# Two operand parts in one 512-column product, output groups of 256 columns, halves summed at evacuation

## The chip, the cores and the metric

The kernel runs on one core of a Trainium2 chip. The metric is the device time of one execution, in microseconds (us), as a median of several runs. TensorE (PE) does the matrix products, VectorE (DVE) and ScalarE (ACT) everything elementwise, GpSimd (POOL) a few small things, and SyncE (SP) issues most of the transfers.

## The reference, cut to what matters

Three transformer blocks run in sequence on one sequence of 256 tokens with 2048 features: two layers of `first_block` and one block of a second kind. Each block has a mixer and a feed-forward part, with a norm and a residual around each:

```python
h = rmsnorm(x, g_pre_mix[l])
proj = h @ w_in[l]                      # 2048 x 4608
y_a = conformer_conv(proj[..., :a_end], ...)
y_b = dilated_attention(proj[..., a_end:b_end], cos, sin)
y_c = pool_mixer(proj[..., b_end:], ...)
y = concat(rms_normalize(y_a), rms_normalize(y_b), rms_normalize(y_c)) * g_mix[l]
x = x + rmsnorm(y @ w_out[l], g_post_mix[l])
h = rmsnorm(x, g_pre_ffn[l])
f = (silu(h @ w_gate[l]) * (h @ w_up[l])) @ w_down[l]      # hidden 5632
x = x + rmsnorm(f, g_post_ffn[l])
```

The third block has the same form with other branches (a linear recurrent unit, a gated delta rule, spatial gating, a short convolution) and a feed-forward part with a convolution of three taps. All data are float32, and the weights (some 590 MB) are read from HBM once.

## The kernel before

**Layout.** Activations lie with features on partitions and 256 tokens along the free axis. A float32 product is made of three products of reduced-precision parts: every weight and every operand is split into a high and a low part, and hi x hi, hi x lo and lo x hi are added up in PSUM. `mms` (L332) does this for one weight tile of 128 x 128: three products of 256 columns (L340, L341, L342), each with a weight load of its own (the first two load the same weights).

**Weights.** `Stream` (L58) cuts the weights into chunks of 512 x 512, each in two halves of 256 rows by 512 columns (512 KB; rows of 2 KB in DRAM). For each half chunk SP issues a load (L79), ACT rounds it to the high part (L87), DVE subtracts to get the low part (L95). `ahead` emits this three half chunks before the products want it; the low parts rotate through four buffers.

**Groups.** `groupA` (L364) computes 512 output features: four tiles of 128 x 256, two in each of two PSUM banks, over its chunks. With K = 2048 a group has 8 half chunks; in the mixer's output products (`oc`, `oa`) it has only 2, in `ob` 4. `dualA` (L404) runs two such groups together at the start of each half block; `groupB` (L385) has tokens on the output's partitions and products of 512 columns (L396 to L398).

**Work beside the products.** All engines follow one order of emission, and each engine takes its own instructions in that order. After every half chunk `pump` (L154) emits work from generators, with a credit of `BUDGET` = 1450 ns of VectorE time per half chunk; what is not used is lost, what is overdrawn is carried on. First come the `hot` generators, then the evacuations of finished groups (`evq`, in order), then the background generators `bg` in their order, each as long as credit is left. A generator yields the time of what it has just emitted; a negative value rests until the next half chunk. `new_ps` (L355) emits, before a new group, whatever is left of the evacuations up to two groups back. `drain` (L195) emits all that is left of the evacuations and of the named generators at once, with no products in between.

**The mixer of a Block1 layer** (L845) runs `dualA` for a and gate, then `pool`, `v0`, `q0`, `q1`, `k0`, `k1`, `v1` (8 half chunks each), `oc` (4 groups), `drain(conv)` (L911), `oa` (4 groups, operand yA), `drain(at)` (L914), `ob` (4 groups, operand yb). Beside them run `conv_gen` (31 taps, then `ln_gen` L571, then `y_gen` L601, which writes yA), `pool_gen`, two `rot_gen`, and `attn_gen` (L731): eleven steps of 900 ns of credit each, one a half chunk at most, each with the reductions of pair s, the scaling of s - 1, the transposes of s - 2 and the product with the values of s - 3. `attn_gen` stands ahead of `conv_gen` in `bg`.

**Feed forward** (`ffn_run` L1027): eleven hidden groups with a gate and an up product, and three passes of down products over hidden groups 0 to 3, 4 to 7 and 8 to 10; `act` (L1048) emits what is left of the evacuation of a hidden group when its product is due. `last_group` and `fin_last` (L935, L957) end a half block with the sums for the norm.

Of the kernel before, what the change touches and what calls it, by code (L numbers as in the profile page):

```python
# [17 lines left out]
P = 128  # L18
# [13 lines left out]
class Params:  # L32
    """Columns of the packed per-feature parameters: name -> (first, count)."""
# [27 lines left out]
class Stream:  # L61
    """Weight chunks of 512 rows by 512 columns, loaded ahead by halves and split into two 12-bit parts."""
# [4 lines left out]
    def __init__(self, net, plan):  # L67
        self.net, self.plan = net, plan
        self.n = 2 * len(plan)
        self.nd = self.nhi = self.nlo = 0  # L70
        self.i = 0
        self.st, self.hi, self.lo = {}, {}, {}

    def _dma(self):
        h = self.nd
        net = self.net
        ap = self.plan[h // 2][1][256 * (h % 2):256 * (h % 2) + 256, :]
        t = net.wst.tile([P, 2, 512], F32, tag="st", name="st")
        net.nc.sync.dma_start(out=t, in_=ap.rearrange("(k p) c -> p k c", p=P))  # L79
        self.st[h] = t  # L80
        self.nd += 1

    def _hi(self):
        h = self.nhi
        net = self.net
        hi = net.whl.tile([P, 2, 512], F32R, tag="hi", name="whi", bufs=self.SA + 2)
        net.nc.scalar.copy(hi, self.st[h])  # L87
        self.hi[h] = hi
        self.nhi += 1

    def _lo(self):
        h = self.nlo
        net = self.net
        lo = net.whl.tile([P, 2, 512], F32R, tag="lo", name="wlo", bufs=self.SA + 1)
# [4 lines left out]
    def ahead(self, i):  # L99
        """Everything emitted that the products of half chunk i and those soon after it want."""  # L100
# [10 lines left out]
    def get(self, key, b):  # L111
        i = self.i
        assert self.plan[i // 2][0] == key and i % 2 == b, (self.plan[i // 2][0], key, i, b)
        self.ahead(i)
        self.i += 1
        return self.hi.pop(i), self.lo.pop(i)


class Net:
    def __init__(self, ctx, tc, ins, out, taps=None):  # L120
# [16 lines left out]
        self.lag = 0  # L137
# [12 lines left out]
    # Generators emit a few instructions and yield their VectorE time in ns, less the TensorE time that  # L150
    # they add; a negative value rests until half a chunk of products later.
# [33 lines left out]
    def flush(self, gid=None):  # L185
        """Emit all that is left of the evacuations up to group `gid`."""
# [8 lines left out]
    def drain(self, *gens):  # L195
        """Emit all that is left of these background generators (of all, if none is named)."""
# [12 lines left out]
    def after(self, gen, ev):  # L209
        """The evacuation `ev`, once the background generator `gen` is through."""  # L210
        def e(ps):
# [6 lines left out]
            yield from ev(ps)  # L218
# [8 lines left out]
    def setup(self):  # L227
        """First what the first products want: a gain, and rows of x in turn with the first weights."""
# [33 lines left out]
    def stat_mm(self, ps, accs, start=True, stop=True):  # L262
        """Sums over features of [128, 256] tiles, tokens on partitions, into ps[:, 0:2]."""
# [5 lines left out]
    def stat(self, accs, n, name="r"):  # L269
        """rsqrt(sum over features / n + eps), tokens on partitions: [128, 2]."""  # L270
# [21 lines left out]
    def rsqrt_fast(self, src, scale, n, name="r"):  # L292
        """The same from ScalarE's square root and one Newton step, where the products wait for it."""
# [11 lines left out]
    def load_sqrt(self):  # L305
        """ScalarE's table of square roots, before it is wanted."""
# [3 lines left out]
    def bcast(self, r, name="R"):  # L310
        """[128 tokens, 2] -> PSUM [128, 256], the same row on every partition."""
# [20 lines left out]
    def mms(self, ps, j, hi, lo, k, act, first, last):  # L332
        """One 128x128 weight tile times 256 tokens, features on the output's partitions."""
        nc = self.nc
        if len(ps) == 2:
            o, head, tail = ps[j // 2][:, j % 2, :], j % 2 == 0, j % 2 == 1
        else:
            o, head, tail = (ps[0][:, j, :], j == 0, j == 1) if j < 2 else (ps[j - 1], True, True)
# [4 lines left out]

    def mms_first(self, ps, hi, lo, acts):
        """The first half chunk's products, in the order in which their operands are ready."""
# [9 lines left out]
    def new_ps(self, shape=(P, 2, T)):  # L355
        self.gid += 1
        self.flush(self.gid - 2 - self.lag)
        self.lag = 0
# [5 lines left out]
    def groupA(self, keys, act, evac=None, now=None):  # L364
        """Chunks `keys` (4 row tiles each) of one 512-column group; act(k) -> (hi, lo).

        evac(ps): generator over both pairs of output tiles; now(j, ps): at once, when output tile j is
        complete (tiles 0 and 1 share a bank and are complete together: j = 1)."""
        ps = self.new_ps()
        if now:  # L370
            ps = [ps[0], ps[1][:, 0, :], self.bank("ps_mm", (P, 2, T))[:, 0, :]]
        nh = 2 * len(keys)
        for h in range(nh):
            hi, lo = self.W.get(keys[h // 2], h % 2)
            for j in range(4):
                for k in range(2):
                    self.mms(ps, j, hi, lo, k, act(2 * h + k), h == 0 and k == 0, h == nh - 1 and k == 1)
                if now and h == nh - 1 and j:
                    now(j, ps[j - 1])
            if evac and h == nh - 1:  # L380
                self.later(evac(ps))
# [1560 lines left out]
```

## Time and profile before

| | us |
|---|---|
| median of 3 runs (lowest, highest) | 3457.39 (3457.18, 3462.28) |
| span of the profiled execution | 3458.9 |
| PE busy | 3423.8 |
| PE weight loads (beside the products) | 3365.6 |
| DVE busy | 2180.8 |
| ACT busy | 1648.5 |
| POOL busy | 105.0 |
| HBM traffic, mean | 176 GB/s |

The profiled execution's span is 1.5 us above the median. The end of a product in the profile is modelled and products overlap, so the cost of one is read from the distance of their starts. A DVE or ACT instruction overlaps its neighbour by some 0.07 us in the same way.

### The profile page before, as it was taken

How to read it: one execution, taken by the hardware profiler on the slowest of the kernel's cores; microseconds unless marked ns; L12 is line 12 of the kernel's file. 1: busy time of each engine (PE TensorE's matmuls, PEld its weight loads, DVE VectorE, ACT ScalarE, POOL GpSimd, SP SyncE). 2: the span in 40 equal slices, each digit the busy share in tenths (PEclk: the TensorE clock that was granted, in tenths of full speed). 3: DMA queues.
4: the chain of work that ended last, by engine and by line, in shares of the span. 5: the costliest groups of instructions: out<-in, count | busy, mean ns of one | idle time of the engine just before them, and what ended most of it. 6: DMA issues, size and time to landing. Idle time of an engine off the chain costs nothing.

```text
span 3458.9 us, 66199 instructions
## 1 busy us (share of the span) xinstructions
PE 3423.8 (99%) x27758; PEld 3365.6 (97%) x27758; DVE 2180.8 (63%) x2957; ACT 1648.5 (48%) x2219; POOL 105.0 (3%) x301
## 2 busy tenths in 40 slices
PE   9999999999999999999999999999999999999999
PEld 9989999999999998999999999999999999999998
DVE  6877755455555787775545555578665766466465
ACT  5556544444344555554444334455435554455344
POOL 0000000000000000000000000001110000000000
PEclk9999999999999999999999999999999999999999
DMA  7654566666665565456666666565435665666563
GB/s 234 185 170 142 169 184 183 184 183 184 183 183 182 162 190 164 157 157 186 183 183 181 186 183 183 178 189 165 128 122 190 179 184 184 183 183 182 185 184 130
DMA packets 315436, 609.44 MB, mean 176 GB/s; under 512 B 19168, under 2 KB 24672, under 8 KB 314880
## 3 DMA queue, kind: packets, MB, share of 16 engines
q1 hardware_dynamic: 314224, 599.37, 57.9%
q0 software_dynamic: 912, 5.83, 0.5%
q8 instruction: 217, 3.56, 0.4%
q14 instruction: 83, 0.68, 0.1%
HBM read 598.84 MB, written 6.29 MB: 175 GB/s over the span
## 4 chain that ended last, share of the span: by engine, by line
PE 95%; DVE 2%; POOL 1%; DMA 1%; issue 0%; ACT 0%; SPq 0%; DVEq 0%; POOLq 0%; ACTq 0%
PE ps_mm L340 29%; PE ps_mm L342 29%; PE ps_mm L341 29%; PE ps_st L266 1%; PE ps_mm L352 1%; PE ps_mm L396 1%; PE ps_mm L397 1%; PE ps_mm L398 1%; PE ps_sc L747 0%; PE ps_av L794 0%; DVE wlo L95 0%; PE ps_pt L782 0%; PE ps_bc L314 0%; POOL q L287 0%; POOL q L286 0%
## 5 line engine op out<-in xcount | busy, mean ns | idle before, releaser
L95 DVE TENSOR_TENSOR wlo<-st,whi 128x1024 fp32r<-128x1024 f32 x1120 | 1365.8, 1222 | 923.0 <-PE ps_mm L342 839.4
L87 ACT CAST whi<-st 128x1024 fp32r<-128x1024 f32 x1120 | 1170.5, 1049 | 1250.7 <-PE ps_mm L341 1084.6
L340 PE MATMUL ps_mm<-hhi,whi 128*128 128x256 f32 x5712 | 1621.0, 284 | 0.1
L341 PE MATMUL ps_mm<-hlo,whi 128*128 128x256 f32 x5712 | 1616.6, 283 | 0.1
L342 PE MATMUL ps_mm<-hhi,wlo 128*128 128x256 f32 x5712 | 1616.5, 283 | 0.3 <-DVE wlo L95 0.3
L340 PEld LDWEIGHTS ps_mm<-hhi,whi 128*128 128x128 f32 x5712 | 1096.5, 192 | 1.2 <-issue 0.3
L341 PEld LDWEIGHTS ps_mm<-hlo,whi 128*128 128x128 f32 x5712 | 1096.5, 192 | 0.6 <-DVE hlo L480 0.3
L342 PEld LDWEIGHTS ps_mm<-hhi,wlo 128*128 128x128 f32 x5712 | 1096.4, 192 | 0.6 <-DVE wlo L95 0.5
L340 PE MATMUL ps_mm<-hid,whi 128*128 128x256 f32 x2112 | 597.9, 283 | 0.0
L342 PE MATMUL ps_mm<-hid,wlo 128*128 128x256 f32 x2112 | 597.7, 283 | 0.0
L341 PE MATMUL ps_mm<-hid,whi 128*128 128x256 f32 x2112 | 597.7, 283 | 0.0
L340 PEld LDWEIGHTS ps_mm<-hid,whi 128*128 128x128 f32 x2112 | 405.5, 192 | 0.0
L341 PEld LDWEIGHTS ps_mm<-hid,whi 128*128 128x128 f32 x2112 | 405.5, 192 | 0.0
L342 PEld LDWEIGHTS ps_mm<-hid,wlo 128*128 128x128 f32 x2112 | 405.5, 192 | 0.0
L342 PE MATMUL ps_mm<-y,wlo 128*128 128x256 f32 x448 | 127.4, 284 | 3.8 <-DVE wlo L95 3.8
L340 PE MATMUL ps_mm<-y,whi 128*128 128x256 f32 x448 | 129.9, 290 | 0.0
L341 PE MATMUL ps_mm<-y,whi 128*128 128x256 f32 x448 | 127.3, 284 | 0.0
L340 PEld LDWEIGHTS ps_mm<-y,whi 128*128 128x128 f32 x448 | 86.4, 193 | 4.8 <-issue 2.0
L342 PEld LDWEIGHTS ps_mm<-y,wlo 128*128 128x128 f32 x448 | 86.5, 193 | 4.2 <-DVE wlo L95 4.2
L341 PEld LDWEIGHTS ps_mm<-y,whi 128*128 128x128 f32 x448 | 86.6, 193 | 0.1
L1019 ACT CAST hid<-su 128x512 fp32r<-128x512 f32 x66 | 40.7, 621 | 88.0 <-DVE su L1018 88.0
L474 ACT ACTIVATE hhi<-x,par 128x256 fp32r<-128x256 f32 x84 | 38.2, 501 | 91.9 <-DVE x L468 91.0
(413 smaller groups left out, 2672.7 us busy)
## 6 DMA issues: line engine op xcount, KB each, us to landing
st<-in_w_in_dram SPq DMA_DIRECT2D x232, 512.0 KB
st<-in_w_gate_dram SPq DMA_DIRECT2D x176, 512.0 KB
st<-in_w_up_dram SPq DMA_DIRECT2D x176, 512.0 KB
st<-in_w_down_dram SPq DMA_DIRECT2D x176, 512.0 KB
st<-in_ffn_up_dram SPq DMA_DIRECT2D x176, 512.0 KB
st<-in_w_out_dram SPq DMA_DIRECT2D x96, 512.0 KB
st<-in_ffn_down_dram SPq DMA_DIRECT2D x88, 512.0 KB
xpark<-x POOLq DMA_DIRECT2D x1, 2048.0 KB, 6.9
```

What stands on the lines that cost most here:

```text
L87: net.nc.scalar.copy(hi, self.st[h])
L95: net.nc.vector.tensor_tensor(lo, self.st.pop(h), self.hi[h], ALU.subtract)
L266: self.nc.tensor.matmul(ps[:, t:t + 1], a[:, t * P:(t + 1) * P], self.ones[:, 0:1], start=start and i == 0 and t == 0, stop=stop and i == ...
L340: nc.tensor.matmul(o, hi[:, k, w], act[0], start=first and head, stop=False)
L341: nc.tensor.matmul(o, hi[:, k, w], act[1], start=False, stop=False)
L342: nc.tensor.matmul(o, lo[:, k, w], act[0], start=False, stop=last and tail)
L352: mm(ps[j // 2][:, j % 2, :], w[:, k, j * P:(j + 1) * P], acts[k][a], start=n == 0 and k == 0 and j % 2 == 0, stop=False)
L396: nc.tensor.matmul(ps[t], a[0][:, ts], hi[:, k, :], start=h == 0 and k == 0, stop=False)
L397: nc.tensor.matmul(ps[t], a[0][:, ts], lo[:, k, :], start=False, stop=False)
L398: nc.tensor.matmul(ps[t], a[1][:, ts], hi[:, k, :], start=False, stop=h == nh - 1 and k == 1)
L474: nc.scalar.activation(hhi[:, k, :], x[:, k, :], AF.Identity, scale=self.p(g, k))
L1019: nc.scalar.copy(h[:, 0, sl, :], u[:, sl, :])
```

## The change

Wherever `groupA` runs, the high weights now meet both parts of the operand at once: one product of 512 columns writes hi x hi into the first half of a bank and hi x lo into the second; lo x hi is a product of 256 columns added to the second half. Each output tile of 128 features so takes a whole bank, a group has 256 output features instead of 512 (two tiles, two banks, half the half chunks), and the evacuation adds the two halves: two ACT copies of 128 x 256, a rest until the next half chunk, two DVE additions of 128 x 256. `dualA`, `groupB` and the very last 256 columns of each half block keep products of 256 columns. The half chunks of `groupA` become 512 rows by 256 columns (rows of 1 KB in DRAM, the same 512 KB). The operand's parts are stored side by side per row tile. Evacuations run pair by pair with rests in them; `hid_gen` rests between the copy of the high part and the subtraction. `BUDGET`, the order of the stages, the drains and the generators of conv, pool, attention and the delta rule are as before.

```diff
+def by_cols(chunks):
+    return [(key, c, ap[:, 256 * c:256 * c + 256], 4) for c in range(2) for key, ap in chunks]

+    def mms_wide(self, o, j, hi, lo, k, act, first, last):
+        mm = self.nc.tensor.matmul
+        w = slice(j * P, (j + 1) * P)
+        mm(o, hi[:, k, w], act[2], start=first, stop=False)
+        mm(o[:, T:], lo[:, k, w], act[0], start=False, stop=last)

+    def take(self, dst, src):
+        if not isinstance(src, list):
+            nc.scalar.copy(dst, src)
+            yield 50
+            return
+        for j in range(2):
+            nc.scalar.copy(dst[:, j, :], src[j][:, 0:T])
+        yield 50
+        yield -1
+        for j in range(2):
+            nc.vector.tensor_tensor(dst[:, j, :], dst[:, j, :], src[j][:, T:], ALU.add)
+        yield 850
+
+    def scaled(self, dst, src, R):
+        if isinstance(src, list):
+            yield from self.take(dst, src)
+            src = dst
+        self.nc.vector.tensor_tensor(dst, src, self.b2(R, dst.shape[1]), ALU.mult)
+        yield 600
+
+    def added(self, dst, src):
+        if not isinstance(src, list):
+            V.tensor_tensor(dst, dst, src, ALU.add)
+            yield 600
+            return
+        for c in (slice(0, T), slice(T, 2 * T)):
+            for j in range(2):
+                V.tensor_tensor(dst[:, j, :], dst[:, j, :], src[j][:, c], ALU.add)
+            yield 850

     def groupA(self, keys, act, evac=None, now=None):
-        ps = self.new_ps()
...
+        n = len(keys)
+        for c in range(2):
+            one = now is not None and c == 1
+            ps = self.new_ps((P, 512))
...
+            for h in range(n):
+                hi, lo = self.W.get(keys[h], c)
+                for j in range(2):
+                    for k in range(4):
+                        mms(ps[j], j, hi, lo, k, act(4 * h + k), h == 0 and k == 0, h == n - 1 and k == 3)
...
+                if h == n - 1 and not one:
+                    self.later(evac(c, ps))
+                self.pump()

     def hk(self, k):
-        return self.hhi[:, k, :], self.hlo[:, k, :]
+        h, k = self.h[k // 8], k % 8
+        return h[:, k, 0, :], h[:, k, 1, :], h[:, k, :, :]

-        def ev_c(cg):
-            def ev(ps):
-                for i in range(2):
-                    nc.scalar.copy(self.f[:, 4 * cg + 2 * i:4 * cg + 2 * i + 2, :], ps[i])
-                    yield 50
-        def ev_a2(cg):
-            def ev(ps):
-                for i in range(2):
-                    o = self.f[:, 4 * cg + 2 * i:4 * cg + 2 * i + 2, :]
-                    V.tensor_tensor(o, o, ps[i], ALU.add)
-                    yield 600
+        ev_c = lambda cg: (lambda i, src: self.take(fpair(cg, i), src))
+        ev_a2 = lambda cg: (lambda i, src: self.added(fpair(cg, i), src))

+    def hid_gen(self, hid, j, i, u, s):
+        V.tensor_tensor(u, u, s, ALU.mult)
+        nc.scalar.copy(h[:, 0, sl, :], u)
+        yield 600
+        yield -1
+        V.tensor_tensor(h[:, 1, sl, :], u, h[:, 0, sl, :], ALU.subtract)
+        yield 600
```

## Rows read from the trace of the kernel before

**Rows 1.** The page, busy time and share of the span, instructions.
```profile
PE 3423.8 (99%) x27758; PEld 3365.6 (97%) x27758; DVE 2180.8 (63%) x2957; ACT 1648.5 (48%) x2219; POOL 105.0 (3%) x301
```
**Rows 2.** Groups of TensorE by line and shape: count, busy us, mean ns | idle before.
```profile
L340 PE MATMUL ps_mm<-hhi,whi 128*128 128x256 f32 x5712 | 1621.0, 284 | 0.1
...
L340 PE MATMUL ps_mm<-hid,whi 128*128 128x256 f32 x2112 | 597.9, 283 | 0.0
...
L340 PE MATMUL ps_mm<-y,whi 128*128 128x256 f32 x448 | 129.9, 290 | 0.0
...
L340 PE MATMUL ps_mm<-yb,whi 128*128 128x256 f32 x256 | 72.9, 285 | 0.0
...
L340 PE MATMUL ps_mm<-yA,whi 128*128 128x256 f32 x64 | 18.1, 283 | 0.0
```
**Rows 3.** Timeline at 1000 us, products of 256 columns: start us, us, instruction.
```profile
1000.10 0.28 PE L340 MATMUL ps_mm<-hhi,whi 128*128 128x256 f32 x1
...
1000.46 0.28 PE L340 MATMUL ps_mm<-hhi,whi 128*128 128x256 f32 x1
```
**Rows 4.** Timeline at 85 us, products of 512 columns (`groupB`), seven apart.
```profile
84.72 0.39 PE L396 MATMUL ps_mm<-whi,hhi 128*128 128x512 f32 x1
...
86.31 0.39 PE L397 MATMUL ps_mm<-wlo,hhi 128*128 128x512 f32 x1
```
**Rows 5.** Groups by line and shape, 195 to 300 us; the last of the page.
```profile
L805 DVE TENSOR_TENSOR yacc<-yacc,ysq 128x256 f32<-128x256 f32 x6 | 2.6, 425 | 2.7 <-ACT ysq L804 2.7
...
L804 ACT ACTIVATE ysq<-ps_av 128x256 f32<-128x256 f32 x6 | 2.3, 385 | 3.5 <-DVE yb L799 3.5
...
L618 DVE TENSOR_TENSOR cs<-cs,ps_bc 128x1024 f32<-128x1024 f32 x1 | 1.2, 1215 | 0.0
...
L609 DVE TENSOR_TENSOR yacc<-yacc,t 128x512 f32<-128x512 f32 x1 | 0.7, 693 | 0.1
L607 ACT ACTIVATE yacc<-cs 128x512 f32<-128x512 f32 x1 | 0.6, 630 | 0.4 <-DVE cs L596 0.4
...
L95 DVE TENSOR_TENSOR wlo<-st,whi 128x1024 fp32r<-128x1024 f32 x1120 | 1365.8, 1222 | 923.0 <-PE ps_mm L342 839.4
```
**Rows 6.** Timeline of PE, one attention step's products between those of `oa`.
```profile
267.23 1.08 PE L794 MATMUL ps_av<-ring,v 128*64 128x256 f32 x8
268.25 1.09 PE L782 MATMUL ps_pt<-ident,ring 128*128 128x128 f32 x8
269.27 1.13 PE L747 MATMUL ps_sc<-k,q 64*128 64x256 f32 x8
```
**Rows 7.** Timeline of DVE, the first instructions of three attention steps.
```profile
269.27 0.17 DVE L768 RECIPROCAL as<-as 128x4 f32<-128x4 f32 x1
269.48 1.14 DVE L772 TENSOR_SCALAR ring<-ring,as 128x256 f32<-128x256 f32 x4
...
275.62 0.18 DVE L768 RECIPROCAL as<-as 128x4 f32<-128x4 f32 x1 [1.02 <-ACT ring L762]
...
282.11 0.17 DVE L768 RECIPROCAL as<-as 128x4 f32<-128x4 f32 x1
```
**Rows 8.** The chain that ended last, stretches of it: start us, us, what.
```profile
55.88 0.80 PE ps_st L266 x8
...
62.79 0.71 PE ps_bc L314 x4
```
**Rows 9.** The chain at the end of the conv branch in layer 0.
```profile
223.27 1.07 ACT cs L595
...
224.37 1.23 DVE cs L596
225.59 1.14 DVE wlo L95
```
**Rows 10.** Stretches (us): busy PE, PEld, DVE, ACT, POOL, clock, DMA share, GB/s.
```profile
14.00:15.00 1.00, 1.00 (x11) 1.00 (x10) 1.00 (x2) 0.78 (x1) 0.00 (x0) 1.00 1.08 383
...
357.00:362.00 5.00, 4.79 (x27) 4.77 (x28) 4.25 (x11) 1.36 (x3) 0.00 (x0) 0.65 0.00 0
...
600.00:750.00 150.00, 150.00 (x1252) 150.00 (x1251) 69.95 (x63) 61.55 (x65) 0.00 (x0) 1.00 0.62 184
...
2342.00:2365.00 23.00, 23.00 (x194) 23.00 (x194) 22.93 (x30) 11.74 (x15) 0.00 (x0) 1.00 0.55 161
```

More of the change, by code (lines that the diff above doesn't have):

```diff
@@ L217, in e @@
                 self.drain_only(gen)
-            yield from ev(ps)
+            yield from ev(*src)
         return e
@@ L364, in groupA @@
     def groupA(self, keys, act, evac=None, now=None):
-        ps = self.new_ps()
[L370 to L381, printed above, removed]
-            self.pump()
+        n = len(keys)
+        for c in range(2):
+            one = now is not None and c == 1
+            ps = self.new_ps((P, 512))
+            if one:
+                ps = [b[:, 0:T] for b in ps]
+            mms = self.mms_one if one else self.mms_wide
+            for h in range(n):
[3 more added lines that the diff above has]
+                        mms(ps[j], j, hi, lo, k, act(4 * h + k), h == 0 and k == 0, h == n - 1 and k == 3)
+                    if one and h == n - 1:
+                        now(j, ps[j])
+                if h == n - 1 and not one:
+                    self.later(evac(c, ps))
+                self.pump()
         return self.gid
@@ L428, in dualA @@
                     if end:
-                        self.evq.append((gids[s], (evac0, evac1)[s](ps[s])))
+                        ev = (evac0, evac1)[s]
+                        for pair in range(2):
+                            self.evq.append((gids[s], ev(pair, ps[s][pair])))
                     self.pump()
-        self.lag = 1
+        self.lag = [1, 1]
         return gids
@@ L687, in qk_evac, with ev @@
     def qk_evac(self, dst, base):
-        nc = self.nc
-        def ev(ps):
-            for i in range(2):
-                k = base + 2 * i
-                nc.vector.tensor_tensor(dst()[:, k:k + 2, :], ps[i], self.b2(self.R), ALU.mult)
-                yield 600
+        def ev(i, src):
+            k = base + 2 * i
+            yield from self.scaled(dst()[:, k:k + 2, :], src, self.R)
         return ev
@@ L937, in last_group, with ev @@
         nc = self.nc
-        if cg < 3:
-            def ev(ps):
-                for i in range(2):
-                    k = 4 * cg + 2 * i
-                    add(self.f[:, k:k + 2, :], ps[i])
-                    self.sq_add(self.f[:, k:k + 2, :], nc.vector)
-                    yield 1200
-                    self.gains(k)
-            self.groupA(keys, act, self.after(gen, ev) if gen else ev)
-        else:
+        def ev(i, src):
+            k = 4 * cg + 2 * i
+            yield from add(self.f[:, k:k + 2, :], src)
+            self.sq_add(self.f[:, k:k + 2, :], nc.vector)
+            yield 600
+            self.gains(k)
+        if cg == 3:
             self.load_sqrt()
-            self.groupA(keys, act, now=lambda j, ps: self.fin_last(j, ps, add))
+        self.groupA(keys, act, self.after(gen, ev) if gen else ev,
+                    now=(lambda j, ps: self.fin_last(j, ps, add)) if cg == 3 else None)
     def gains(self, upto):
@@ L1053, in act @@
                     self.flush(gids[j])
-                return hid[j][:, 0, k % 4, :], hid[j][:, 1, k % 4, :]
+                return self.yk(hid[j], k % 4)
             def ev(cg):
-                def e(ps):
-                    for i in range(2):
-                        o = f[:, 4 * cg + 2 * i:4 * cg + 2 * i + 2, :]
-                        if first:
-                            nc.scalar.copy(o, ps[i])
-                            yield 50
-                        else:
-                            V.tensor_tensor(o, o, ps[i], ALU.add)
-                            yield 600
-                return e
-            add = lambda o, ps: V.tensor_tensor(o, o, ps, ALU.add)
+                to = self.take if first else self.added
+                return lambda i, src: to(f[:, 4 * cg + 2 * i:4 * cg + 2 * i + 2, :], src)
             for cg in range(4):
@@ L1361, in ba_gen @@
         yield -1
-        ps = self.bank("ps_ba")[:, 0:T]
+        ps = self.bank("ps_ba")
         for k in range(KD):
```

430 lines of the change are left out of this document (200 added, 230 removed).

## The prediction

> **What bounds the kernel now.** I read the page first: PE is busy 99% of the span, DVE 63%, ACT 48% [rows 1]. So the question is what one product costs. The groups of TensorE show that nearly all of PE's work is the three lines of `mms`, with almost no idle time before them [rows 2]; the duration there is modelled, so I go to the timeline. Three products of 256 columns take 0.36 us from start to start, 0.120 each [rows 3]. In `groupB` the same kernel runs products of 512 columns: seven take 1.59 us, 0.227 each [rows 4]. Twice the columns cost 107 ns more, so a product of 256 columns has 107 ns of columns and 13.3 ns (120 - 107) that come once per product whatever its width. That fixed part is what the change can save. Then I read who waits for whom: DVE's weight split waits 839 us in all for PE to give back a buffer [rows 5]. DVE is thus held about one half chunk ahead of PE by the four buffers, and work that `pump` emits after half chunk i runs about while PE does half chunk i. Last I read the stretches of the mixers, where DVE is nearly full or where drains stand.
>
> **What the change saves.** A weight tile goes from 3 x 0.120 = 0.360 us to 0.227 + 0.120 = 0.347 us: one fixed part of 13.3 ns less, the columns being the same 768. The tiles of `mms` are 5712 + 2112 + 448 + 256 + 64 = 8592 [rows 2]. Not changed are the tiles of the six `dualA` (128 tiles each, 48 of them in `mms_first`, so 720 here) and of the last 256 columns of each half block (72 of hid, 32 of yb, 16 of y and yA: 120). That leaves 7752 tiles x 13.3 ns = **103 us**. The weight loads stay hidden: at 512 columns they have more cover than now.
>
> Here the Trainium skill speaks against the change. "TensorE: Matmul & The Clock Gate", section "Back-to-back issue gap", puts a product at N / 2.4 + 2.5 ns, 109 ns for 256 columns and 216 for 512, so the fixed part would be 2.5 ns and the saving 19 us. The rows differ from it (120 and 227), and the sum goes by the rows.
>
> **Evacuations.** Each pair of tiles gets two DVE additions of 128 x 256 more, 2 x 0.425 us, and ACT copies at about 0.385 each [rows 5]. `groupA` evacuates 292 pairs in all (98 in each of the two layers, 96 in the third block), of which 6 are narrow: 286 x 0.85 = 243 us more on DVE. 2181 + 243 over about 3400 is 71% of the span, so over the whole DVE does not become the bound. In the feed forward it is at 47% [rows 10] and has room: no cost there. In the mixers the extra work is not a matter of busy time but of credit.
>
> **The drains of the Block1 mixers.** The pump gives 1450 ns per half chunk. An evacuated pair in `pool`, `q0`, `q1`, `k0`, `k1` now costs 50 + 850 + 600 = 1500 instead of 600: ten pairs, 9000 ns, over six half chunks of credit, and conv is last in the queue. Its taps so end about 8 half chunks later, at the end of `v1`. In `oc` (8 half chunks, 11,600 ns) the eight pairs cost 900 each instead of 50, 7200; attention is next and gets four steps (3600), where it gets eight now; conv gets the rest, overdrawn. At `drain(conv)` 4800 ns of conv are left: the tanh, and all of `y_gen`. In `oa` the eight pairs want 1700 each, 13,600 against 11,600: attention gets nothing, and at `drain(at)` seven of its eleven steps are left. Before, the same count gives a conv that ends one half chunk before `oa` and an attention that ends with the last half chunk of `oa`; the attention steps in the trace stand where this count puts them, one or two half chunks apart [rows 6, 7]. `oa` needs yA, `ob` needs yb, and a drain emits no products, so what is drained stands in PE's way.
>
> *drain(conv)*, from the last product of `oc`: ACT copies of the last pair 0.77 (they wait for that product and stand before the tanh in ACT's queue); tanh 1.07 and DVE 1.23 [rows 9]; two squares 1.26, their sum 0.69 [rows 5]; sums on PE, GpSimd's inverse root and the broadcast 62.79 + 0.71 - 55.88 = 7.62 [rows 8]; DVE 1.22 [rows 5]; the first high and low part, about 1.0. Sum 14.9 us, of which 1.5 is PE's own work that it does today too: 13.4 us idle. After a shorter pause, PE's clock was granted at 0.65 in the mean over 5 us, between the levels of 1.2 and 2.4 GHz, and 27 products took 4.79 us instead of 3.24 [rows 10]: 1.6 more. **15 us** a layer.
>
> *drain(at)*: first the last pair's four additions, 4 x 0.425 = 1.7. A step cannot be faster than its own loop (scale on DVE, reduce on DVE, exponentials on ACT, next scale): the steps' first instructions lie 6.35 and 6.49 us apart where PE had only some 6.0 of work [rows 7]. Four of the seven steps have this loop, 25.6 us; then scale 1.35, transposes 1.09, copies 1.2, values 1.08 for the last pair, 4.7. Sum 32.0. PE's own part is 3.1 for a full step [rows 6], 4 x 3.1 + 2 x 2.1 + 1.05 = 17.6, which it does today too. Idle 14.4, restart 1.6: **16 us** a layer. Both drains in two layers: **62 us**. Today the end of conv (ACT 1.07, DVE 1.23) holds back a weight split and PE for some 2 us a layer [rows 9]; that wait goes into the drain: -3.7.
>
> **Smaller terms.** (a) The last down pass has three half chunks per group, and hidden group 10 is wanted at the third, two after its evacuation began (now four). With the new rests the subtraction is still to be emitted, behind a weight split that waits for PE: 1.2 [rows 5] + 0.7 less 0.7 of products before it, about 1.3 in two halves; with the convolution four taps, a product, a copy and a subtraction, about 4: **7 us**. (b) In the third block, DVE is full at 2342 to 2365 [rows 10]. Two pairs more there (1.7) and a stage 3.7% shorter (0.9) have to show: 2.6, and as much beside it; taken as **5**, ends 0 and 12. (c) Sums and broadcast lie two half chunks apart, 5.55 us instead of 5.76, against 6.1 needed [rows 8]: **2**. (d) Rows of 1 KB: the loads of x are such rows, and at 14 to 15 us they landed at 383 GB/s [rows 10]; the stream takes 184, about 190 after: no cost, covered by the buffers ahead. If that cover went, DMA would bound at far more than this rate, so nothing is added.
>
> The split of a moving operand into two stretches of 256 columns (for y and hid) is not in the trace. Bounds: 0 as in [rows 4], or a whole fixed part, which would take the 103 us back. I take 0, since the columns still come one after another into one bank.
>
> **Sum** against the profiled execution: 3458.9 - 103 + 62 - 3.7 + 7 + 5 + 2 = 3428. The median lies 1.5 below that execution: **3427 us**, 0.9% faster, where the products alone would give 3.0%.
>
> **Rivals.** *The drains are mostly hidden.* For it: DVE and ACT run ahead of PE, and the chain may begin while the last group's products run. Against it: both begin behind evacuations that wait for PE's last product. With a third of the 62 left the time is 3457 - 103 + 21 + 10 = 3385. Chance 0.25 for 3360 to 3404.
>
> *The drains cost more than the products save.* The mechanism: with no products between them PE's clock falls, the steps' own products take twice as long and come into the loop, and the splits that follow are late. The point is 47 us a layer for both drains instead of 31; at 56 the time is 3478. For it: the clock row [rows 10]. Against it: 3.1 us of a step's 6.4 is PE's, beside the loop. Chance 0.09.
>
> *The product of 512 columns doesn't save what it should*: the fixed part is paid per 256 columns of the moving operand. Then nothing is saved and the time is 3457 + 72 = 3529. Against it: [rows 4]. Chance 0.03. A milder form, in which the fixed part is only some 2.5 ns and most of the 13.3 goes with the columns, saves 19 and gives 3457 - 19 + 72 = 3510; [rows 3, 4] speak against it too. Chance 0.02. This milder form is the rule of the Trainium skill's "TensorE: Matmul & The Clock Gate" cited above.
>
> *No change that can be measured* (some 0.2%, 7 us, is what a measurement of this kernel can tell): drains at about 45 a layer, 3450 to 3464. Chance 0.09. My forecast, 3405 to 3450, has 0.52.
>
> **How the numbers follow.** Faster 0.52 + 0.25 = 0.77; same 0.09; slower 0.14. The range leaves out the lower end of the first rival and most of the slower cases: 3372 to 3470.
>
> **What would show it.** Starts of PE in a wide group 0.227 and 0.120 apart, 2 per tile (right), or 0.24 (wrong). In each Block1 mixer two idle stretches of PE: 13 us before the first product with yA, and before the first with yb some 32 us with attention products alone. If these are shorter than 5 us, my count of credit or of cover is wrong and the time lies near 3385; if PE idles for DVE's splits through the mixers, the additions were not hidden. In the feed forward no new wait but one of a few us before hidden group 10.

## The result and the profile after

The changed kernel takes 3514.1 us (median of 4 runs, 3506.47 to 3522.86) against 3457.28 before (4 runs, 3455.14 to 3462.28). The ratio is 1.0158, 95% interval 1.0134 to 1.0181: slower by 1.6%, where 0.9% faster was forecast, and outside the range of 3372 to 3470. The profiled execution has a span of 3504.8 us.

The page of after, busy time of each engine with its share of the span, and then its groups of instructions (busy us, mean ns | idle time before them and what ended it), answering [rows 1] and [rows 2, 5]:

```profile
span 3504.8 us, 51460 instructions
PE 3384.7 (97%) x19942; PEld 2962.4 (85%) x19942; DVE 2394.8 (68%) x3604; ACT 1757.0 (50%) x2608; POOL 106.3 (3%) x301
...
L96 DVE TENSOR_TENSOR wlo<-st,whi 128x1024 fp32r<-128x1024 f32 x1120 | 1365.3, 1223 | 716.9 <-PE ps_mm L367 490.9
L366 PE MATMUL ps_mm<-h,whi 128*128 128x512 f32 x4992 | 1763.9, 398 | 0.0
L367 PE MATMUL ps_mm<-h,wlo 128*128 128x256 f32 x4992 | 1402.1, 281 | 6.3 <-DVE wlo L96 6.3
L366 PE MATMUL ps_mm<-hid,whi 128*128 128x512 f32 x2040 | 718.8, 397 | 7.3 <-DVE hid L1063 7.3
L366 PE MATMUL ps_mm<-y,whi 128*128 128x512 f32 x440 | 161.9, 409 | 4.7 <-DVE y L688 4.7
```

TensorE is idle 120 us now (3504.8 - 3384.7), 35 before (3458.9 - 3423.8). VectorE has 214 us more to do (2394.8 against 2180.8 in [rows 1]; 243 were forecast).

The product pairs (a pair of products is here the one of 512 and the one of 256 columns of one weight tile) come at two paces. The timeline of TensorE (start, modelled duration), first in the first block's feed forward, then in the third block's, answering [rows 3, 4]:

```profile
999.72 0.40 PE L366 MATMUL ps_mm<-h,whi 128*128 128x512 f32 x1
999.96 0.28 PE L367 MATMUL ps_mm<-h,wlo 128*128 128x256 f32 x1
1000.08 0.40 PE L366 MATMUL ps_mm<-h,whi 128*128 128x512 f32 x1
1000.32 0.28 PE L367 MATMUL ps_mm<-h,wlo 128*128 128x256 f32 x1
1000.43 0.40 PE L366 MATMUL ps_mm<-h,whi 128*128 128x512 f32 x1
...
3099.91 0.39 PE L366 MATMUL ps_mm<-h,whi 128*128 128x512 f32 x1
3100.14 0.28 PE L367 MATMUL ps_mm<-h,wlo 128*128 128x256 f32 x1
3100.26 0.39 PE L366 MATMUL ps_mm<-h,whi 128*128 128x512 f32 x1
3100.49 0.28 PE L367 MATMUL ps_mm<-h,wlo 128*128 128x256 f32 x1
3100.60 0.39 PE L366 MATMUL ps_mm<-h,whi 128*128 128x512 f32 x1
```

Two pairs take 0.71 us in the first stretch and 0.69 in the second. To see it precisely, take a whole pass of down products (32 half chunks of 8 pairs): 90.5 us in the first two blocks and 88.7 in the third, so 353.3 or 346.7 ns a pair. The second is the forecast's 347; the first saves half as much. The 0.24 from a product of 512 columns to the next start, which the prediction named as the sign of a wrong price, stands in the first stretch. The windows of the same kernel (stretch, its length, then busy us and count of PE, PEld, DVE, ACT, POOL, and the granted clock) say that no clock is behind it: it is full in both.

```profile
600.00:700.00 100.00, 100.00 (x568) 86.73 (x567) 54.10 (x62) 44.44 (x56) 0.00 (x0) 1.00 0.58 186
3100.00:3200.00 100.00, 100.00 (x579) 88.16 (x578) 74.66 (x106) 56.16 (x82) 0.00 (x0) 1.00 0.62 188
```

What TensorE waited for, in four stretches of after: from `oc` to the first products with yb in the first layer; the end of `ob`; gq to gz of the third mixer (the four input groups of its delta rule); the last down pass of the third block (total us, times, longest). Here ps_av is attention's product with the values, ps_st are the sums for a norm, ps_bc is the broadcast of its factor, sqacc are the squares that the closing norm sums up:

```profile
PE ps_av L851 <- ACT ring L841: 10.8, 6, 2.7
PE ps_st L278 <- DVE yacc L671: 6.6, 1, 6.6
PE ps_bc L326 <- POOL r_y L301: 4.0, 1, 4.0
PE ps_mm L366 <- DVE y L688: 2.4, 1, 2.4
...
PE ps_st L278 <- DVE sqacc L583: 5.7, 1, 5.7
...
PE ps_mm L367 <- DVE wlo L96: 5.5, 2, 3.4
PE ps_st L278 <- DVE yacc L671: 5.3, 1, 5.3
...
PE ps_mm L366 <- DVE hid L1063: 4.8, 1, 4.8
```

The three waits ahead of the first yA product (6.6 + 4.0 + 2.4) are the drain of conv, the ps_av waits that of attention. From the last product with yA to the first with yb 34.9 us pass in each layer, with attention's products alone, where the prediction named some 32. The other two places were not in the forecast, or far too small there.

**The account.** I took the start of every half chunk from both traces (narrow: three products of 256 columns per weight tile; wide: one of 512 and one of 256) and split each stage's time into a nominal part (2.880 us per narrow half chunk, 2.720 in `groupB`, 2.773 per wide one), the excess of wide half chunks that run at 2.827, and the rest, "stalls" (waits, other products, and half-clock stretches behind a wait). The sum closes on the spans' difference of 45.9 us:

| us, after less before | forecast | measured |
|---|---|---|
| products at 346.7 ns a pair | -103 | -103.4 |
| the part of them that ran at 353.3 | 0 | +31.6 |
| `oc` and `oa`, two layers (drains less the old conv stall) | +58 | +67.6 (32.9 and 34.7) |
| last down passes (hidden group 10) | +7 | +8.6 (1.1, 1.4, 6.1) |
| third mixer | +5 | +23.2 (17.7 of it in gq to gz) |
| `ob`, two layers | 0 | +17.2 (8.7 and 8.5) |
| everything else | +2 | +0.9 |
| sum | -31 | +45.7 |

### The profile page after: what moved, and what is told of

It is laid out like the page before. It is cut to its first block, busy times and chain, and to the rows that moved or that the text cites. A ratio compares the mean times of both kernels' runs of the same rounds, so it can differ in the third digit from the quotient of the medians.

```text
span 3504.8 us, 51460 instructions
## 1 busy us (share of the span) xinstructions
PE 3384.7 (97%) x19942; PEld 2962.4 (85%) x19942; DVE 2394.8 (68%) x3604; ACT 1757.0 (50%) x2608; POOL 106.3 (3%) x301
## 4 chain that ended last, share of the span: by engine, by line
PE 88%; DVE 6%; POOL 2%; ACT 2%; issue 1%; DMA 0%; SPq 0%; DVEq 0%; POOLq 0%; ACTq 0%
PE ps_mm L366 48%; PE ps_mm L367 24%; PE ps_mm L350 2%; PE ps_mm L351 2%; PE ps_mm L349 2%; DVE wlo L96 2%; PE ps_mm L460 1%; PE ps_mm L461 1%; PE ps_mm L462 1%; POOL q L298 1%; PE ps_st L278 1%; PE ps_mm L413 1%; POOL q L299 1%; PE ps_bc L326 1%; ACT ring L819 0%
## 5 line engine op out<-in xcount | busy, mean ns | idle before, releaser
L366 PE MATMUL ps_mm<-h,whi 128*128 128x512 f32 x4992 | 1763.9, 398 | 0.0
L367 PE MATMUL ps_mm<-h,wlo 128*128 128x256 f32 x4992 | 1402.1, 281 | 6.3 <-DVE wlo L96 6.3
L366 PEld LDWEIGHTS ps_mm<-h,whi 128*128 128x128 f32 x4992 | 938.9, 188 | 224.9 <-issue 0.3
L367 PEld LDWEIGHTS ps_mm<-h,wlo 128*128 128x128 f32 x4992 | 944.9, 189 | 7.5 <-DVE wlo L96 7.4
L366 PE MATMUL ps_mm<-hid,whi 128*128 128x512 f32 x2040 | 718.8, 397 | 7.3 <-DVE hid L1063 7.3
L366 PEld LDWEIGHTS ps_mm<-hid,whi 128*128 128x128 f32 x2040 | 384.1, 188 | 99.7 <-DVE hid L1063 8.3
L349 PE MATMUL ps_mm<-h,whi 128*128 128x256 f32 x720 | 204.4, 284 | 0.1
L350 PE MATMUL ps_mm<-h,whi 128*128 128x256 f32 x720 | 204.2, 284 | 0.1
L351 PE MATMUL ps_mm<-h,wlo 128*128 128x256 f32 x720 | 204.0, 283 | 0.0
L366 PE MATMUL ps_mm<-y,whi 128*128 128x512 f32 x440 | 161.9, 409 | 4.7 <-DVE y L688 4.7
L402 DVE TENSOR_TENSOR f<-f,ps_mm 128x256 f32<-128x256 f32 x272 | 101.5, 417 | 68.8 <-PE ps_mm L367 63.6
L349 PEld LDWEIGHTS ps_mm<-h,whi 128*128 128x128 f32 x720 | 138.4, 192 | 0.3 <-ACT h L541 0.3
L350 PEld LDWEIGHTS ps_mm<-h,whi 128*128 128x128 f32 x720 | 138.3, 192 | 0.3 <-DVE h L547 0.3
L351 PEld LDWEIGHTS ps_mm<-h,wlo 128*128 128x128 f32 x720 | 138.1, 192 | 0.0
L366 PEld LDWEIGHTS ps_mm<-y,whi 128*128 128x128 f32 x440 | 85.1, 193 | 27.5 <-DVE y L688 5.3
```

What stands on the lines that cost most here:

```text
L349: nc.tensor.matmul(o, hi[:, k, w], act[0], start=first and head, stop=False)
L350: nc.tensor.matmul(o, hi[:, k, w], act[1], start=False, stop=False)
L351: nc.tensor.matmul(o, lo[:, k, w], act[0], start=False, stop=last and tail)
L366: mm(o, hi[:, k, w], act[2], start=first, stop=False)
L367: mm(o[:, T:], lo[:, k, w], act[0], start=False, stop=last)
L402: V.tensor_tensor(dst[:, j, :], dst[:, j, :], src[j][:, c], ALU.add)
```

## The experiments

Every kernel below ran beside the kernel before on the same chip; stalls are counted as in the account.

**e1_ffn_wide: wide products in the feed forwards only.**

```diff
-    self.groupA(keys("pool"), self.hk, self.pool_evac(l))     # and all other mixer groups but the last 512 features
+    self.groupN(keys("pool"), self.hk, self.pool_evac(l))     # 512 columns, mms, evac(i, ps[i]) of one narrow pair
```

> The mixers' output groups are narrow again (512 columns, three products of 256, one evacuation); the products of 512 columns stay in the feed forwards and in the last 512 features of each half block. Theory 1 (the stalls that the change brought sit in the mixers, and the products do save): the mixers' stalls return to those of before, about 110 of the 117 us; 735 half chunks of the feed forwards save 0.107 us each at a pace of 2.773 us (78 us), or 0.053 where PE runs at the pace of 2.827 us seen in the first two blocks; hidden group 10 costs 9. Time 3387 if all of it runs at 2.773, 3412 with the paces as in the profile of after, 3427 with 2.827 everywhere. Theory 2 (the wide products slow the rest down, by traffic of operands or of PSUM, wherever they stand): the feed forwards themselves would bring nothing and the time is 3450 or more.

Measured: 3439.3 us (median of 9, 3414.46 to 3452.26), ratio 0.994 (0.9919 to 0.9962). The profiled run, 3414.46, had nearly all its pairs at the fast pace (2.7 us lost, 31.6 in after), and stalls 30.3 us above before instead of 117.5. So most of the stalls sit in the mixers, as theory 1 had it: `oc` and `oa` together are within 1 us of before, the ends of `ob` at +3 a layer, the last down passes at +8. One place did not go back: gq to gz still has +12.0 with narrow groups. And the times of one and the same program spread over 38 us. The lowest, 3414, lies 27 above the all-fast 3387 of theory 1; 22 of this are stalls that I had not expected there, most of them in gq to gz and `ob`. The spread is as large as the pace can make it (735 half chunks at 0.0533 us are 39), but the paces of the other eight runs were not seen.

**e4_credit: the kernel before, with only the credit charged as after.**

```diff
     nc.vector.tensor_tensor(dst()[:, k:k + 2, :], ps[i], self.b2(self.R), ALU.mult)
-    yield 600
+    yield 1500          # pool too; oc 50 -> 900, oa 600 -> 1700
```

> The kernel before, with its own narrow products and evacuations; only the credit charged for an evacuated pair is raised to what the changed kernel charges (1500 in pool, q and k, 900 in oc, 1700 in oa). No instruction is added or removed. By the count, 4800 ns of conv and 6300 ns of attention are left at the two drains, the same as in the changed kernel. Theory 1 (the drains come from the order of emission that the credit sets): oc and oa together take some 30 us more in each layer, 3457 + 55 to 65 = 3512 to 3522. Theory 2 (the drains come from VectorE's added instructions): at most 10 us more, 3457 to 3467.

Measured: 3529.1 us, ratio 1.0207 (1.0192 to 1.0222). `oc` and `oa` grow by 32.8 and 35.2 us, as in after (32.9 and 34.7), the other stages stay within 2 us, and the waits of the same stretch are the same four:

```profile
PE ps_av L794 <- ACT ring L784: 10.4, 5, 3.8
PE ps_st L266 <- DVE yacc L609: 6.9, 1, 6.9
PE ps_bc L314 <- POOL r_y L289: 4.1, 1, 4.1
PE ps_mm L340 <- ACT y L622: 1.9, 1, 1.9
```

No instruction was added. The drains are made by the order of emission that the credit sets: theory 1, and the count of credit in the prediction.

**e3_budget: more credit.**

```diff
     ev_a, ev_g = self.conv_evacs()
+    self.BUDGET = 2450.0      # 1450 again behind ob
```

> The changed kernel with a credit of 2450 instead of 1450 ns per half chunk in the two mixers of the first kind. By the count of credit, conv then ends 25 half chunks before its drain and attention with the last half chunk of oa, as before the change. Theory 1 (the drains come from the credit alone): the idle stretches ahead of the first yA and yb products vanish, 66 us less, and the evacuations behind ob are emitted in time, some 10 us less: 3435 to 3450. Theory 2 (the credit only shows that VectorE, 91% busy in q and k, has no more room): the weight splits behind it come late, PE waits for them through q, k and v1, and of the 66 us at most a third is won: 3490 to 3515.

Measured: 3502.5 us, ratio 1.0133 (1.0114 to 1.0152): the time of theory 2, though each theory was right about a part. The drains do vanish (`oc` and `oa` at 2.7 and 0.8 us below before). The ends of `ob`, where theory 1 expected 10 us less, do not: they stand 10.6 and 9.7 us above before, 8.7 and 8.5 in after. And v0 and q to k are 34.6 and 35.4 us above it, and all stalls together are 121.4 us above before, 117.5 in after. The waits from v0 to v1, the one at the end of `ob` in the first layer, and the window of q to k with its granted clock of 0.90:

```profile
PE ps_bc L326 <- POOL r_y L301: 9.6, 2, 6.0
PE ps_mu L641 <- DVE cs L629: 5.9, 1, 5.9
PE ps_st L278 <- DVE yacc L671: 2.4, 2, 2.1
PE ps_mm L461 <- DVE wlo L96: 2.1, 4, 0.7
...
PE ps_st L278 <- DVE sqacc L583: 7.8, 1, 7.8
...
104.00:226.00 122.00, 103.23 (x535) 88.03 (x534) 94.97 (x150) 60.87 (x99) 16.05 (x36) 0.90 0.49 153
```

TensorE waits less for weight splits (2.1) than theory 2 said; it is the small products of the chains, queued in its order, that wait for a VectorE that is behind. So the credit is not an idle rule. It stands for VectorE's time, which in after was busy for 84.5 of the 93 us of q and k; with more of it the same work is only late in another place.

**e9_no_adds: the additions left out.**

```diff
     yield 50
     yield -1
-    for j in range(2):
-        nc.vector.tensor_tensor(dst[:, j, :], dst[:, j, :], src[j][:, T:], ALU.add)
-    yield 850
...                                # in `added` the two additions of the second half likewise
```

> The changed kernel with its wide products and its rests, but the second half of every bank is left out of the sum (the hi x lo and lo x hi parts are computed and not added), and the credit for it is not charged. Theory 1 (VectorE's additions and their credit make the drains and the ends): oc and oa return to within 6 us of before in each layer, the ends of ob to within 3, the third mixer falls by half; of the 117 us of stalls 20 to 35 remain, and the time is 3375 to 3400 with the fast pace, up to 3432 with the slow one. Theory 2 (the new order of evacuation, pair by pair with rests, makes them): more than 60 us of stalls remain, 3420 to 3460.

Measured: 3401.6 us (3395.73 to 3411.02), ratio 0.9841 (0.9817 to 0.9866), with 17.1 us of slow pace in the profiled run. Stalls fall from +117.5 to +32.8. `oc` and `oa` together are within 1 us of before in each layer; in the stretch where after has four waits, one of 0.4 us is left:

```profile
PE ps_bc L326 <- POOL r_b L301: 0.4, 1, 0.4
```

So the additions, with their credit, are the reason for which the drains come. The wait for hidden group 10 is gone in the first two blocks and 2.7 us instead of 4.8 in the third. Not explained by the additions: +12.4 in gq to gz, and +5 at each end of `ob`. The third mixer as a whole falls from some 23 us above before to 18 only, where theory 1 had expected half.

**e6_again and e2_hi_then_lo: where the slow pace comes from.** First the changed kernel again, unaltered:

> The changed kernel once more, unaltered, to see which of its stretches run at which pace in another execution. Theory 1 (the pace of 353 or 347 ns per pair is chosen at a restart): stalls and drains are the same as in the profile of after within 2 us, other stretches are fast or slow than there, and the times fall between 3478 (all fast) and 3521 (all slow). Theory 2 (the pace belongs to the first two blocks): the same stretches are slow, and the times do not leave 3504 to 3523.

Measured: 3496.7 us (3482.19 to 3506.03), ratio 1.0101 (1.0078 to 1.0123). Stalls are 120.2 us above before (117.5 in after, 2.7 apart where theory 1 said 2), but now the first feed forward is fast and the other two are slow. The windows:

```profile
600.00:700.00 100.00, 100.00 (x579) 88.19 (x578) 54.49 (x61) 45.07 (x57) 0.00 (x0) 1.00 0.58 190
1700.00:1800.00 100.00, 100.00 (x569) 86.68 (x568) 58.37 (x69) 46.21 (x59) 0.00 (x0) 1.00 0.56 185
3100.00:3200.00 100.00, 100.00 (x568) 86.67 (x567) 74.18 (x107) 54.99 (x81) 0.00 (x0) 1.00 0.60 185
```

So theory 1: theory 2 would have had the same stretches slow. As long as pairs follow one another, with no wait and no other product in between, the pace does not change; in after it turned at a wait of 0.8 us for a weight split in the third feed forward and turned back at hidden group 10. A wait is not needed: in the mixers 7 of the 33 turns in after stand where only other products came in between and TensorE did not wait. With 969 wide half chunks at 0.0533 us the pace alone is worth up to 52 us, and the eight runs of this program lie within 41 us of each other.

```diff
-    for k in range(4):
-        mms(ps[j], j, hi, lo, k, act(4 * h + k), ...)                     # 512, 256, 512, 256, ...
+    for k in range(4):
+        mm(ps[j], hi[:, k, w], act(4 * h + k)[2], ...)                    # four of 512
+    for k in range(4):
+        mm(ps[j][:, T:], lo[:, k, w], act(4 * h + k)[0], ...)             # four of 256
```

> The changed kernel with another order of the same products: for each output tile and half chunk four products of 512 columns, then four of 256, instead of one and one in turn. Theory 1 (the slow pace of 353 ns per pair comes from the alternation of the two lengths, PE falling 16 cycles of 2.4 GHz behind at one of the two changes): with a quarter of the alternations the loss falls to a quarter or less; a half chunk takes 2.773 to 2.787 us in all three blocks, and the time is 3514 less 20 to 40, 3474 to 3494. Theory 2 (the pace belongs to the place of the operands or to the traffic of the first two blocks, not to the order): half chunks of 2.827 us stay in the first two feed forwards, and the time stays 3504 to 3523.

Measured: 3506.2 us, ratio 1.0137 (1.012 to 1.0154), runs only 3.5 us apart. All three feed forwards run at 2.807 us a half chunk, 350.8 ns a pair. Neither theory fits whole: the place of the operands is out (the third block is no faster), and the order matters; but the loss is not a quarter, it has become the same everywhere.

**e5_paces: the products by themselves.** The blocks are of 144 to 288 products, more than the expectation says.

```diff
+    if pat == "alt":  seq += [m for p in zip(H, L) for m in p]       # 512, 256 in turn
+    if pat == "hllh": seq += [H[0], L[0], L[1], H[1], H[2], L[2], L[3], H[3]]
+    if pat == "wide": seq += H + H[:2]                               # 512 alone; "narrow": 256 alone
```

> A probe, not the network: everything is left out but products on one set of operands, in 31 blocks of 72 to 192 products each, with a pause of ScalarE copies before every block and nothing else running on VectorE, GpSimd or the queues. Blocks: one 512 and one 256 in turn (pauses of about 2 to 9 us, 15 times), the same with the operand's parts apart as in y and hid, 512-256-256-512, four 512 then four 256, 512 alone with the activations moving and with the weights moving, 256 alone, and 512-256 with the second product in the bank's first half. Theory 1 (two paces of one instruction stream, chosen when TensorE starts again): the blocks of one 512 and one 256 in turn run at 347 ns a pair in some and 353 in others, constant within a block, with no other engine at work; 512 alone 227 to 233, 256 alone 120. Theory 2 (the slow pace is traffic from VectorE, ScalarE or the transfers): all those blocks run at 347 and 512 alone at 227.

Measured, from the starts within the blocks, at full clock but for the last row (many blocks began with a few us at a granted clock of 0.50):

| order | ns per pair (or product) |
|---|---|
| 512, 256 in turn, 15 blocks | 346.7 in 11, 353.3 in 4 |
| the same, operand parts apart, or second product in the first half of the bank, 4 blocks | 346.7 |
| 512, 256, 256, 512, 2 blocks | 348.3 |
| four of 512, four of 256, 2 blocks | 350.8 |
| 512 alone (activations or weights moving, 6 blocks) | 226.7 |
| 256 alone, 2 blocks | 120.0 |
| 512, 256 in turn, at a granted clock of 0.50 | 640 |

A fast and a slow block of 512 and 256 in turn: two starts that lie 30 pairs apart, 10.40 us in the one and 10.60 in the other, and a window of 28 us of each:

```profile
93.06 0.39 PE L77 MATMUL alt<-h,hi 128*128 128x512 f32 x1
...
103.46 0.39 PE L77 MATMUL alt<-h,hi 128*128 128x512 f32 x1
...
139.80 0.40 PE L77 MATMUL alt<-h,hi 128*128 128x512 f32 x1
...
150.40 0.40 PE L77 MATMUL alt<-h,hi 128*128 128x512 f32 x1
...
92.00:120.00 28.00, 27.92 (x162) 24.36 (x160) 0.00 (x0) 0.00 (x0) 0.00 (x0) 1.00 0.00 1
128.00:156.00 28.00, 28.00 (x160) 24.28 (x159) 0.00 (x0) 0.00 (x0) 0.00 (x0) 1.00 0.00 1
```

No other engine is at work, the clock is full, and the paces still differ. So the two paces belong to TensorE and this order, and not to traffic: theory 1. Blocks behind a pause of 2.1 us ran at either pace, and so did blocks behind 4.0; what decides, at a restart or behind other products, stays open. So does why the same 512 and 256 columns cost 346.7, 348.3, 350.8 or 353.3 ns by their order alone. The difference of 6.7 ns is 16 periods of 2.4 GHz; that is arithmetic and explains nothing.

**e7_hllh: an order with one pace.** The mixers narrow as in e1_ffn_wide, and in the feed forwards:

```diff
-        mms(ps[j], j, hi, lo, k, act(4 * h + k), ...)
+    H(0); L(0); L(1); H(1); H(2); L(2); L(3); H(3)        # H: 512 columns of hi, L: 256 of lo
```

> Narrow groups in the mixers as in e1_ffn_wide, and in the wide groups the order 512-256-256-512 within four row tiles, which the probe ran at 348.3 ns a pair in both of its blocks. Theory 1 (the pace is a matter of the order and of the restart, and this order has one pace): every wide half chunk takes 2.787 us in all three feed forwards, 735 x 0.093 = 69 us saved, some 30 us of stalls as in e1_ffn_wide remain: 3416 to 3425, with a spread of under 8 us between runs. Theory 2 (the two paces come back in the full kernel): a spread from 3415 to 3452 as in e1_ffn_wide, a median near 3440.

Measured: 3421.6 us (3419.85 to 3422.87), ratio 0.9898 (0.988 to 0.9916). Three feed forwards at one pace, in the windows too, and 3 us between the runs where e1_ffn_wide had 38: theory 1, in time and spread. The two kernels below keep this order: all their feed forwards ran at the same pace too, and their runs lie within 6 and 1 us.

```profile
600.00:700.00 100.00, 100.00 (x576) 87.42 (x575) 51.38 (x56) 44.33 (x55) 0.00 (x0) 1.00 0.59 190
1700.00:1800.00 100.00, 100.00 (x576) 87.36 (x575) 51.05 (x57) 43.90 (x56) 0.00 (x0) 1.00 0.58 188
3050.00:3150.00 100.00, 100.00 (x576) 87.31 (x575) 74.41 (x107) 55.40 (x81) 0.00 (x0) 1.00 0.62 189
```

**e8_rests and e10_gelu_rest: the rests.** First three of the new rests taken out:

```diff
     nc.scalar.copy(h[:, 0, sl, :], u)        # hid_gen
     yield 600
-    yield -1
+    if j < 10:
+        yield -1
...                                           # the third mixer's convolutions: no rest behind the copies
     nc.scalar.activation(t, o, AF.Tanh)      # its silu
-    yield -1
+    yield 0
```

> As e7_hllh, and the rests that the change put into the evacuations are taken out in three places: before the subtraction of hidden group 10, and behind the copies of ScalarE in the convolutions and the silu of the third block's mixer. Theory 1 (these rests are what the last down pass and the third mixer wait for): 6 to 8 us less in the last down passes (0.5 to 1 in the first two blocks, 4 to 6 in the third) and 5 to 10 us less in the mixer of the third block: 3404 to 3412. Theory 2 (the stalls there come from evacuating pair by pair and not from the rests): within 4 us of e7_hllh.

Measured: 3423.7 us, ratio 0.9899 (0.9883 to 0.9915): no gain. The last down passes of the first two blocks lose their wait (1.3 and 0.9 us above before in e7_hllh, none here), the third block's does not (5.6 against 4.9), and gq to gz stays 12.5 above before. The stage sc to sb of the third mixer loses its 4.8 us, but su and sv lose the 3.5 that they were below before and gq to gz takes 2.0 more, so the mixer as a whole is no better. In time theory 2; the rests did act, and what they gave back was lost beside them. Then also the rests of one evacuation in the third mixer, the gelu of the recurrent unit's gate:

```diff
     for c in self.gelu_parts(out, t):
         yield c
-        yield -1
```

> As e8_rests, and the two rests in the evacuation of the recurrent unit's gate (gelu, third mixer) are taken out as well. In e8_rests the 16 products ps_ba and some 20 small VectorE steps behind them came at the seventh half chunk of the stage gq to gz, before the evacuations, and PE waited later in the same stage; in the kernel before they came at the 23rd, and PE waited 0.2 us. Theory 1 (these rests let the background work pass the evacuations, and the work put off then meets a full VectorE): ps_ba goes back to the 20th half chunk or later, the stage's stalls fall from 24 us to 12 to 16, and the time from 3424 to 3412 to 3416. Theory 2 (the rests are not it; the stalls come from evacuating pair by pair): within 4 us of 3424.

Measured: 3412.2 us (3411.51 to 3412.48), ratio 0.9866 (0.985 to 0.9883). The `ps_ba` products go back from the 7th half chunk of gq to gz to the 23rd, where before had them (in after they came at the 5th), the stage takes 104.9 us (104.1 before, 118.9 after), and its waits, which in after were 5.5 and 5.3 us, are

```profile
PE ps_st L278 <- DVE yacc L702: 0.6, 1, 0.6
PE ps_bc L326 <- POOL r_pre L301: 0.2, 1, 0.2
```

So theory 1 for this one: two rests in a queue that is emptied in order let the background work go first, some 20 small VectorE steps long. That the work put off then met a VectorE without room fits [rows 10] and e8_rests, where it is busy for 20.8 of the 23 us from 2331 us on while TensorE stands for 6.7; no run shows that step by itself. This kernel is 1.3% faster than before, and faster than both kernels of the case.

## Why the prediction was wrong, point by point

**The saving per product: mechanism right, size wrong.** A weight tile does go to 0.347 us, to 0.3 ns, at one of two paces. The step that failed is the addition of two durations, each read in a row of its like [rows 3, 4], to that of a mixed row that no trace of before shows. e5_paces confirms both durations, 120.0 and 226.7, and shows that mixed rows cost 0 to 6.7 ns more per pair by order and by restart. The term was -103 and measured -72 (-103.4 + 31.6) in the profiled run; it is the largest single error. I had a bound of the right kind, a whole fixed part for the split operand, but tied it to the split, which costs nothing (346.7 with parts apart).

The rule of the Trainium skill ("TensorE: Matmul & The Clock Gate", section "Back-to-back issue gap"), 109 and 216 ns, is given there for an isolated product, and the section says that it does not hold for a stream of products with weight loads; the prediction left that out. The probe, a stream in which nothing else ran, measured 120.0 and 226.7; the measurement decides. The rival drawn from it, 3510, is 4 us from the result for another reason: it had too small a saving and too few stalls.

**The drains: right.** The count of credit gave the backlog, and e4_credit shows that it alone is enough to make the drains. 13 us of idle time before the first yA product were forecast, and 6.6 + 4.0 + 2.4 = 13.0 came. The two layers cost 67.6 us net, 58 forecast. The first rival (drains mostly hidden) is out.

**The ends of `ob`: missing.** I costed no step there. The evacuations lag behind their groups, and the flush puts the last of them between the last products and the sums: 5.7 us of wait for sqacc, 8.6 us of stalls a layer. A pair of tiles costs 2700 of the 2900 credit of its two half chunks, but credit is not what makes the lag: with 2450 a half chunk the wait is 7.8 and 7.3 us (e3_budget). By the order of emission a pair with its rest takes two calls of `pump` at either credit, as many as its group has, so a lag that is there once is not made up; that is read from the code, and no run takes the rest out there. Without the additions 5 remain, and with narrow groups up to the last 512 features 3; the part that belongs to the additions is shown, what makes the rest is open.

**The third mixer: 5 forecast, 23 measured.** I looked at VectorE's full stretch [rows 10] and priced two pairs of additions. What I did not price were the rests, which the description of the change names. Two of them, in one evacuation, make 11.8 us where the mixer's groups are narrow (e8_rests to e10_gelu_rest: 24.5 to 12.7 us of stalls in the stage, 11.9 before). The last 6 of the 17.7 in gq to gz came with the wide groups (17.7 against 12.0 in e1_ffn_wide) and go with their additions (12.4 in e9_no_adds). What the rest of the mixer adds, 5.5 us net, is not taken apart.

**Hidden group 10: size right, cause half right.** 7 forecast, 8.6 measured. In the first two blocks either the rest or the additions, taken out alone, end the wait. In the third the rest is not it (e8_rests); the additions are part of it (4.8 to 2.7).

**Feed forward otherwise and DMA: right; statistics: no cost.** No other new wait of note in the feed forwards; rows of 1 KB cost nothing seen. The broadcast of pool's statistics was forecast to wait 2 us more in both layers. It waits 1.0 us a layer in after, and it waited longer before (first layer):

```profile
PE ps_bc L314 <- POOL r_y L289: 1.4, 1, 1.4
```

The errors add up: 31.6 (pace) + 18.2 (third mixer) + 17.2 (`ob`) + 9.3 (drains) + 0.5 (the remainder, with rounding) is 76.8, the profiled span less the forecast's 3428. Any one of them alone would have left the time inside the range; the range had been widened for the drains only. The median of 3514.1 lies 7.6 us above the time of the profiled run, 3506.5: two of the four runs were 14 to 16 us slower than that one, which one feed forward at the other pace (some 250 half chunks at 0.0533, 13 us) would make; their paces were not seen.

## What to carry to other kernels

A saving per instruction that comes from mixing two kinds has to be measured in the mixed order, in a short probe and at several restarts, before it is multiplied by thousands. Where background work is emitted by a credit that stands for an engine's time, a new instruction costs twice: its time, and the place of everything queued behind it; charge it in each stage by the stage's own spare time, and put wide products with dearer evacuations only where that engine has room (here the feed forwards). A rest in a queue that is emptied in order is a change of order too: price what is let past.

## What the runs showed of the hardware

One stream of alternating 512- and 256-column products, each with a weight load of its own, ran at two paces, 346.7 and 353.3 ns a pair at full clock. Each was kept, for hundreds of microseconds in the feed forwards, until the next wait or other product; the probe had both with nothing else running. At a granted clock of 0.50, which is the level of 1.2 GHz, a pair took 640 ns (e5_paces, 123.58 to 125.50 us, three pairs), less than twice either pace. The order 512, 256, 256, 512 had the one pace of 348.3 in both blocks of the probe and in all three feed forwards of e7_hllh, and its times lay within 3 us of each other (four runs; 6 and 1 in e8_rests and e10_gelu_rest) instead of 38 (nine runs of e1_ffn_wide). What decides between the two paces stays open.
